# Splitting the first load of an unpooling kernel's indices into two DMAs

## The chip, the cores and the metric

The kernel runs on one core of one Trainium2 chip. The metric is device time in microseconds (us), the median of several executions. Two kernels that are compared by a ratio ran side by side on one chip; the experiments used four chips in all (numbers 11, 10, 3 and 9). The profiler's span starts at the first instruction shown and is about 1.3 us shorter than the time (70.2 against 71.51 us in the profiled run of the kernel before).

## The reference

It is a max-unpooling by 2. Each input value goes to one of the four places of a 2 x 2 output block; the index, 0 to 3, says which. The other three places are zero.

```python
x:       (16, 64, 32, 32) float32
indices: (16, 64, 32, 32) integers 0..3   (64-bit when they reach the kernel)
output = zeros((16, 64, 64, 64), float32)
out_i = i * 2 + idx // 2
out_j = j * 2 + idx % 2
output[b, c, out_i, out_j] = x[b, c, i, j]
```

4.19 MB of x and 8.39 MB of indices are read, 16.78 MB are written.

## The kernel before

A partition holds T = 8 images of N = 1024 values. Three loads are issued first, all on SyncE's queue: three images of indices (24 KB per partition), all of x (32 KB), five images of indices (40 KB).

```python
FIRST = 3
cut = FIRST * 2 * N          # an index is two 32-bit words
program.first(
    nc.sync.dma_start(out=idx_t[:, :cut], in_=idx_v[:, :cut]).then_inc(
        idx_in[0], 16
    )
)
program.first(nc.sync.dma_start(out=x_t, in_=x_v).then_inc(x_in, 16))
program.first(
    nc.sync.dma_start(out=idx_t[:, cut:], in_=idx_v[:, cut:]).then_inc(
        idx_in[1], 16
    )
)
```

VectorE waits for x, then for the first indices (and at the fourth image for the others). For each place of the 2 x 2 block one operation computes (index == place) * x, over one or two images (n below). Two images are one group; four groups are stored, one DMA of 4 MB each, again on SyncE's queue. The last group reuses the output buffer of the first, so it waits for the first store.

```python
nc.vector.wait_ge(x_in, 16).then_inc(x_in, -16)
for t in range(T):
    g, k = t // G, t % G
    if t in (0, FIRST):
        half = int(t == FIRST)
        nc.vector.wait_ge(idx_in[half], 16).then_inc(idx_in[half], -16)
    ...
    if g == NG - 1:
        nc.vector.wait_ge(stored_0, 16).then_inc(stored_0, -16)
    ...
    for pidx in range(4):
        op = nc.vector.scalar_tensor_tensor(
            out=o_c[:, k : k + n, :, pidx // 2, :, pidx % 2],
            in0=idx_c[:, t : t + n],
            scalar=pidx,
            in1=x_c[:, t : t + n],
            op0=mybir.AluOpType.is_equal,
            op1=mybir.AluOpType.mult,
        )
    if k + n == G:
        op.then_inc(made, 1)

for g in range(NG):
    nc.sync.wait_ge(made, g + 1)
    nc.sync.dma_start(out=out_v[g], in_=out_t[g]).then_inc(
        stored if g else stored_0, 16
    )
```

Of the kernel before, what the change touches and what calls it, by code (L numbers as in the profile page):

```python
# [1 line left out]

# [4 lines left out]

P = 128
F32 = mybir.dt.float32
I32 = mybir.dt.int32  # L10


class Program:




    def __init__(self, nc):
        self.nc = nc
        self.block = nc.main_func.blocks[0]  # L20
        self.kernel_block = nc.cur_bb.bb.name

    def __enter__(self):
        ins = self.block.instructions
        self.branches = [i for i in ins if "Branch" in type(i).__name__]
        n = len(ins) - len(self.branches)
        assert all("Branch" in type(ins[k]).__name__ for k in range(n, len(ins)))
        del ins[n:]
        self.nc.switch_bb(self.block.name, parent=None)
        self.symbolic = self.nc._always_lower_symbolic_ap  # L30
        self.nc._always_lower_symbolic_ap = False
        return self

    def first(self, made):
        ins = self.block.instructions
        assert ins[len(ins) - 1].name == made.ins.name
        moved = ins.pop()
        at = next(
            k
            for k, i in enumerate(ins)  # L40
            if i.engine == moved.engine and isinstance(i, mybir.InstDrain)
        )
        ins.insert(at, moved)

    def last(self, made):


        def move(nc):
            ins = self.block.instructions
            at = next(k for k, i in enumerate(ins) if i.name == made.ins.name)  # L50
            nc.main_func.blocks[-1].instructions.append(ins.pop(at))

        self.nc.at_finalize(move)

    def __exit__(self, kind, *_):
        self.nc._always_lower_symbolic_ap = self.symbolic
        if kind is None:
            for b in self.branches:
                self.block.instructions.append(b)
            self.nc.switch_bb(self.kernel_block, parent=None)  # L60


@with_exitstack
def kernel(
    ctx: ExitStack,
    tc: tile.TileContext,
    x: bass.AP,
    indices: bass.AP,
    kernel_size: bass.AP,
    out: bass.AP,  # L70
):
    nc = tc.nc
    assert kernel_size == 2

    B, C, H, W = x.shape
    n_img = B * C
    T = n_img // P
    assert T * P == n_img and C % T == 0

    G = 2  # L80
    NG = T // G
    FIRST = 3
    N = H * W
    x_v = x.rearrange("b (ch t) h w -> (b ch) (t h w)", t=T)
    idx_v = indices.rearrange("b (ch t) h w -> (b ch) (t h w)", t=T).bitcast(I32)
    out_v = out.rearrange("b (ch g t) oh ow -> g (b ch) (t oh ow)", g=NG, t=G)

    x_t = nc.alloc_sbuf_tensor("x_t", [P, T * N], F32).ap()
    idx_t = nc.alloc_sbuf_tensor("idx_t", [P, T * 2 * N], I32).ap()
    out_t = [  # L90
        nc.alloc_sbuf_tensor(f"out_t{g}", [P, G * 4 * N], F32).ap()
        for g in range(NG - 1)
    ]
    out_t.append(out_t[0])

    x_in = nc.alloc_semaphore("x_in")
    idx_in = [nc.alloc_semaphore(f"idx_in{g}") for g in range(2)]
    made = nc.alloc_semaphore("made")
    stored_0 = nc.alloc_semaphore("stored_0")
    stored = nc.alloc_semaphore("stored")  # L100

    x_c = x_t.rearrange("p (t i j) -> p t i j", t=T, j=W)
    idx_c = idx_t.rearrange("p (t i j two) -> p t i j two", t=T, j=W, two=2)[
        :, :, :, :, 0
    ]
    cut = FIRST * 2 * N

    with Program(nc) as program:
        program.first(
            nc.sync.dma_start(out=idx_t[:, :cut], in_=idx_v[:, :cut]).then_inc(  # L110
                idx_in[0], 16
            )
        )
        program.first(nc.sync.dma_start(out=x_t, in_=x_v).then_inc(x_in, 16))
        program.first(
            nc.sync.dma_start(out=idx_t[:, cut:], in_=idx_v[:, cut:]).then_inc(
# [6 lines that stand above are left out]
            g, k = t // G, t % G  # L123
            if t in (0, FIRST):
                half = int(t == FIRST)
                nc.vector.wait_ge(idx_in[half], 16).then_inc(idx_in[half], -16)  # L126


            if k == 1 and t != FIRST and g:
                continue  # L130
            n = 1 if k == 1 or t + 1 == FIRST or not g else 2
            if g == NG - 1:
                nc.vector.wait_ge(stored_0, 16).then_inc(stored_0, -16)
            o_c = out_t[g].rearrange(
                "p (m i two j wo) -> p m i two j wo", m=G, two=2, wo=2, j=W
# [18 lines that stand above are left out]
        nc.sync.sem_inc(made, -NG)  # L154
        program.last(
            nc.sync.wait_ge(stored, 16 * (NG - 1)).then_inc(stored, -16 * (NG - 1))
        )


# [1 line left out]
_INS = ['x', 'indices', 'kernel_size']  # L161
_OUTS = [((16, 64, 64, 64), 'float32')]

_NUMBERS = {'kernel_size': 2}


# [26 lines left out]
```

## Time and profile before

| What | Value |
|---|---|
| time, median of 3 runs before the prediction | 71.60 us |
| span of the profiled run | 70.2 us |
| DMA engines: share of 16 engines' span | 97.6% |
| VectorE busy | 35.9 us, 51% |
| bytes moved | 29.36 MB |
| last load landed / last store landed | 31.4 / 70.2 us |

Read it as one queue: loads, then stores, one after the other on the same 16 DMA engines (mean landings at 9.42, 19.13 and 31.25 us for the loads, 40.95 to 69.93 for the stores). The profile's lines stand in the prediction. Besides the views, the prediction and the text below use the trace's single records: each DMA packet with its start, duration and size, and each landing, which is the moment when one of the 16 engines reports that its part of a DMA is done. A DMA has 16 landings (112 for the seven DMAs of the kernel before); "lands at" means the mean of the 16 unless the last is named.

### The profile page before, as it was taken

How to read it: one execution, taken by the hardware profiler on the slowest of the kernel's cores; microseconds unless marked ns; L12 is line 12 of the kernel's file. 1: busy time of each engine (PE TensorE's matmuls, PEld its weight loads, DVE VectorE, ACT ScalarE, POOL GpSimd, SP SyncE). 2: the span in 40 equal slices, each digit the busy share in tenths (PEclk: the TensorE clock that was granted, in tenths of full speed). 3: DMA queues.
4: the chain of work that ended last, by engine and by line, in shares of the span. 5: the costliest groups of instructions: out<-in, count | busy, mean ns of one | idle time of the engine just before them, and what ended most of it. 6: DMA issues, size and time to landing. Idle time of an engine off the chain costs nothing.

```text
span 70.2 us, 76 instructions
## 1 busy us (share of the span) xinstructions
DVE 35.9 (51%) x24; POOL 0.2 (0%) x4
## 2 busy tenths in 40 slices
DVE  0000000000089999999999999999999500000000
POOL 1000000000000000000000000000000000000000
DMA  7699996979988899869999796969799896969692
GB/s 210 294 406 434 448 598 299 560 336 467 504 373 373 373 584 537 373 299 504 392 411 486 317 579 299 598 299 579 317 467 429 373 523 299 598 299 598 299 486 112
DMA packets 1008, 29.36 MB, mean 418 GB/s; under 512 B 112, under 2 KB 112, under 8 KB 112
## 3 DMA queue, kind: packets, MB, share of 16 engines
q1 hardware_dynamic: 1008, 29.36, 97.6%
HBM read 12.58 MB, written 16.78 MB: 418 GB/s over the span
## 4 chain that ended last, share of the span: by engine, by line
DVE 46%; DVEq 4%; issue 1%
DVE out_t L138 46%; DVEq L188 4%
## 5 line engine op out<-in xcount | busy, mean ns | idle before, releaser
L138 DVE SCALAR_TENSOR_TENSOR out_t<-idx_t,x_t 128x1024 f32<-128x1024 int32 (+1 forms) x24 | 35.9, 1574 | 19.6 <-DVEq L126 19.6
L174 POOL MEMSET const-bfloat16-1.0<- 128x1 bf16 x1 | 0.1, 101 | 0.0
L174 POOL MEMSET const-uint8-127<- 128x1 uint8 x1 | 0.1, 101 | 0.0
L174 POOL MEMSET const-float32-0.0<- 128x1 f32 x1 | 0.1, 98 | 0.2 <-issue 0.2
L174 POOL MEMSET const-float32-1.0<- 128x1 f32 x1 | 0.1, 98 | 0.0
## 6 DMA issues: line engine op xcount, KB each, us to landing
out_dram<-out_t SPq DMA_DIRECT2D x4, 4096.0 KB, 13.4
idx_t<-in_indices_dram SPq DMA_DIRECT2D x1, 5120.0 KB, 30.5
x_t<-in_x_dram SPq DMA_DIRECT2D x1, 4096.0 KB, 18.9
idx_t<-in_indices_dram SPq DMA_DIRECT2D x1, 3072.0 KB, 9.6
```

The costliest lines, as they stand in the source:

```text
L138: op = nc.vector.scalar_tensor_tensor(out=o_c[:, k : k + n, :, pidx // 2, :, pidx % 2], in0=idx_c[:, t : t + n], scalar=pidx, in1=x_c[:, t ...
L174: nc = _bacc.Bacc("TRN2", target_bir_lowering=False, num_devices=1)
L188: with _tile.TileContext(nc) as tc:
```

## The change

The intent is that the first data come in smaller pieces. The first load becomes two: one image (8 KB rows) and two images (16 KB rows). Both raise the same semaphore, each by 16, so the wait is for 32.

```diff
-        program.first(
-            nc.sync.dma_start(out=idx_t[:, :cut], in_=idx_v[:, :cut]).then_inc(
-                idx_in[0], 16
+        for part in (slice(0, 2 * N), slice(2 * N, cut)):
+            program.first(
+                nc.sync.dma_start(out=idx_t[:, part], in_=idx_v[:, part]).then_inc(
+                    idx_in[0], 16
+                )
             )
-        )
...
-                nc.vector.wait_ge(idx_in[half], 16).then_inc(idx_in[half], -16)
+                n_in = 16 if half else 32
+                nc.vector.wait_ge(idx_in[half], n_in).then_inc(idx_in[half], -n_in)
```

## The prediction

> **What bounds the kernel now.** I read the page first for the busy shares. VectorE, the only engine that computes, is busy half the span; the 16 DMA engines are busy nearly all of it.
>
> ```profile
> DVE 35.9 (51%) x24; POOL 0.2 (0%) x4
> ...
> DMA packets 1008, 29.36 MB, mean 418 GB/s; under 512 B 112, under 2 KB 112, under 8 KB 112
> ## 3 DMA queue, kind: packets, MB, share of 16 engines
> q1 hardware_dynamic: 1008, 29.36, 97.6%
> ```
>
> What to see: the queue's packets fill 97.6% of 16 engines' span, 0.976 x 70.2 = 68.5 us, so only about 1.7 us of the span is not filled. The page's chain of waits names VectorE for 46%, but it does not follow the data of the stores, which are what ends the program; it is not the chain to work with here.
>
> Second, the issues and their landings, which give the order in which the one queue is worked off.
>
> ```profile
> out_dram<-out_t SPq DMA_DIRECT2D x4, 4096.0 KB, 13.4
> idx_t<-in_indices_dram SPq DMA_DIRECT2D x1, 5120.0 KB, 30.5
> x_t<-in_x_dram SPq DMA_DIRECT2D x1, 4096.0 KB, 18.9
> idx_t<-in_indices_dram SPq DMA_DIRECT2D x1, 3072.0 KB, 9.6
> ```
>
> What to see: the three loads are issued at 0.00, 0.43 and 0.91 us (timeline below) and land at 9.6, 0.43 + 18.9 = 19.3 and 0.91 + 30.5 = 31.4 us. They are worked off one after the other, not side by side: 9.6 us for 3 MB, 9.7 for 4 MB, 12.1 for 5 MB. From the trace's own landing records (mean over the 16 engines), the loads land at 9.42, 19.13 and 31.25 us and the four stores at 40.95, 50.61, 60.28 and 69.93: one store each 9.66 us, which is 4.194 MB / 9.66 us = 434 GB/s, without a hole from 9.4 us on.
>
> Third, the timeline, to see whether the queue ever runs dry because a store is issued late, and how the head looks.
>
> ```profile
> 0.00 0.38 SPq L110 DMA_DIRECT2D idx_t<-in_indices_dram  x1
> ...
> 0.43 0.43 SPq L114 DMA_DIRECT2D x_t<-in_x_dram  x1
> 0.91 0.43 SPq L116 DMA_DIRECT2D idx_t<-in_indices_dram  x1
> 19.56 35.87 DVE L138 SCALAR_TENSOR_TENSOR out_t<-idx_t,x_t 128x1024 f32<-128x1024 int32 x24 [19.56 <-DVEq L126]
> 28.76 27.03 SPq L151 DMA_DIRECT2D out_dram<-out_t  x4
> ```
>
> What to see: VectorE starts at 19.56 us, when x has landed; the first indices landed 10 us before. The first store is issued at 28.76 us, while the last load's packets run until 31.02 us; the next stores are issued at 37.84, 46.65 and 55.46 us (the records behind the merged row), each while the store before still runs. So VectorE has slack and the stores follow the loads without a gap.
>
> Fourth, the single DMA packets in the trace. A packet is one row of one partition: 24,576 bytes take 912 ns, 32,768 take 1213, 40,960 take 1514. A line through the ends is (1514 - 912) / 16384 = 0.0367 ns per byte, plus 912 - 24,576 x 0.0367 = about 9 ns per packet; it gives the 1213 of the middle one too. A semaphore packet of 4 bytes also takes 9 ns, with a gap of 6. Each of 16 engines moves 8 rows of each DMA: 8 x (912 + 1213 + 1514) + 32 x 1213 = 67.93 us, which is 97% of the span. The rest, worked out for the mean engine: its first packet starts at 1.25 us (the first at 1.03, the last at 1.82); that first packet takes on average about 0.54 us more than 912 ns (1.00 to 1.78 us); seven semaphore packets cost 7 x 15 ns = 0.1 us. 1.25 + 0.54 + 67.93 + 0.10 = 69.8, against a measured mean last landing of 69.93. Outside the span lie another 71.6 - 70.2 = 1.4 us, which no kernel edit of this kind touches.
>
> So the kernel is a DMA queue at line rate plus a head of some 1.8 us, and only the head is within reach of this change.
>
> [...]
>
> **The change part by part.** It removes one DMA of 128 rows of 24 KB and adds one of 128 rows of 8 KB and one of 128 rows of 16 KB, same bytes, same place in the queue. The order of instructions on VectorE is unchanged (16 small and 8 large operations); SyncE has one DMA issue more, and the wait for the first indices is for 32 instead of 16.
>
> Per engine, packets: an 8 KB row by my line is 8192 x 0.0367 + 9 = 310 ns (the trace has 8 KB instruction-fetch packets of 307), a 16 KB row 611. 8 x (307 + 611) = 7344 ns against 8 x 912 = 7296: plus 48 ns. One semaphore packet more: plus 15 ns. In the queue: plus 0.06 us, on the path.
>
> SyncE: one issue more of 0.38 to 0.43 us with a 0.05 us gap, so the loads of x and the late indices are issued about 0.45 us later, at about 0.9 and 1.4. Off the path: the first two DMAs give the engines 7.3 us of work from about 1.8 us on, and x is needed in the queue at about 9 us. The barrier that SyncE joins after its issues moves from 1.67 to about 2.1 us; VectorE waits for x until 19.3 anyway. Cost 0.
>
> Between the two halves: the second DMA is issued at about 0.43 us; the engines' first descriptors came 1.03 to 1.82 us after the first issue, so by about 1.5 to 2.3 us the second set is there. The 8 KB rows last until about 1.8 + 2.5 = 4.3 us. No hole.
>
> The head: the first packets' excess of 0.54 us. First packets that start at 1.03 us take 1.7 us, those that start at 1.8 only 1.0; all end at 2.5 to 2.9 us. So the data begins to flow at about 1.6 to 2.0 us on every engine, whenever its record starts, which looks like a start-up that all share and that does not depend on the row. If so the change wins 0 here; if the excess grows with the first row it shrinks to a third, and 0.36 us are won.
>
> Sum: +0.06 us and a possible -0.36 us.
>
> **The rivals.** First, the head shrinks: for it speaks that the excess sits in the first packets alone and that these are the longest of their kind; against it that the late starters have almost no excess (1004 - 912 = 92 ns) at the same 24 KB. Time 71.6 + 0.06 - 0.36 = 71.3. Second, small rows run worse than the line says, say 30 ns more on each of the 16 packets: 71.6 + 0.06 + 0.5 = 72.1; against it the 307 ns record for 8 KB. Third, the first indices come earlier or later and VectorE with them: hidden anyway, since they have 10 us in hand before x, so 0. Fourth, the store chain gets a hole: the first store is issued 2.26 us before the last load's packets end, and it would have to be issued after about 30 us (31.02 less the 1.03 us from issue to first packet) to leave one; both ends of that margin hang on the loads' landing and move together. Time up to 72.5, very unlikely.
>
> **Range and chances.** The central case is 71.66 (no effect in the head), weight about two thirds; the head shrinking, wholly or partly, about 71.3, one third: mean 71.55. The runs before spread 0.1 us, so a range of 71.2 to 71.85 holds both with some noise. To be over 2% faster takes 1.43 us, more than the 0.54 us of excess and most of the head that is issue time and stays; over 2% slower takes a hole that nothing opens. Each 2%.
>
> **What would show it.** Right: packets 1152 (128 data and 16 semaphore packets more), DMA share again near 97 to 98%, first packets 8 KB long with the data beginning at 1.6 to 2.0 us, both halves of the first indices landed by about 9.5 us, VectorE's start near 19.6, the four stores 9.66 us apart, span 70.0 to 70.3. The head shrinks: x lands 0.3 us earlier and every later landing by the same. Small rows costly: 8 KB packets over 330 ns or gaps between them, first indices after 9.8. Wrong altogether: landings between stores that are no longer 9.66 us apart, or a wait of the queue for VectorE.

A paragraph that leaned on general figures and rules, which no trace of this case shows, has been cut from the prediction, and no term of its sum went with it: 71.6 + 0.06 = 71.66 us with a weight of two thirds, 71.6 + 0.06 - 0.36 = 71.3 with one third, mean 71.55. What went with it is the argument that nothing is to be won in the middle of the queue. Shown are the 434 GB/s per store and 67.93 us of packets in a span of 70.2; that no faster rate exists was not. That the wait for 32 is safe is shown only as a correct result of the changed kernel, in its run beside the experiments.

Where the prediction and the expectations say that a DMA's descriptors come or are there, read that its packets can start: the records show packets alone, and in the kernel before the first ones started 1.03 to 1.82 us after the first issue. When the second DMA's packets can start is the estimate from that.

## The result

The changed kernel took 71.54 us (6 runs, 71.43 to 71.62), the kernel before 71.57 us (6 runs). The ratio is 0.9996, with a 95% interval of 0.9983 to 1.001. Ratios here are the mean time of one kernel's runs over that of the other's of the same rounds, so they are not quite the ratio of the medians quoted. The measured time lies 0.01 us from the predicted 71.55 us, and "within 2%" held.

The page of the changed kernel, queue view:

```profile
DMA packets 1152, 29.36 MB, mean 418 GB/s; under 512 B 128, under 2 KB 128, under 8 KB 128
## 3 DMA queue, kind: packets, MB, share of 16 engines
q1 hardware_dynamic: 1152, 29.36, 97.6%
```

There are 144 packets more, the 128 data packets and 16 semaphore packets that were forecast, at the same bytes, mean rate and share. Next, the issues: what, issuing queue, how many, KB each, us from issue to landing.

```profile
out_dram<-out_t SPq DMA_DIRECT2D x4, 4096.0 KB, 13.5
idx_t<-in_indices_dram SPq DMA_DIRECT2D x1, 5120.0 KB, 30.1
x_t<-in_x_dram SPq DMA_DIRECT2D x1, 4096.0 KB, 18.4
idx_t<-in_indices_dram SPq DMA_DIRECT2D x1, 2048.0 KB, 9.1
idx_t<-in_indices_dram SPq DMA_DIRECT2D x1, 1024.0 KB, 4.7
```

and the timeline of the changed kernel (start us, duration us, engine, line, operation):

```profile
0.00 0.86 SPq L111 DMA_DIRECT2D idx_t<-in_indices_dram  x2
...
0.90 0.43 SPq L115 DMA_DIRECT2D x_t<-in_x_dram  x1
1.38 0.65 SPq L117 DMA_DIRECT2D idx_t<-in_indices_dram  x1
19.50 35.87 DVE L140 SCALAR_TENSOR_TENSOR out_t<-idx_t,x_t 128x1024 f32<-128x1024 int32 x24 [19.50 <-DVEq L128]
28.70 27.03 SPq L153 DMA_DIRECT2D out_dram<-out_t  x4
```

The loads are issued 0.47 us later, and the shorter times from issue to landing (18.4 for 18.9 us, 30.1 for 30.5) are only that. In absolute time nothing moved:

| lands at (mean of 16), us | before | after |
|---|---|---|
| first image of indices | - | 4.50 |
| all first indices | 9.42 | 9.39 |
| x | 19.13 | 19.11 |
| other indices | 31.25 | 31.24 |
| stores | 40.95, 50.61, 60.28, 69.93 | 40.93, 50.60, 60.27, 69.92 |
| very last landing | 70.16 | 70.18 |

### The profile page after: what moved, and what is told of

Read it like the earlier page. It is cut to its first block, busy times and chain, and to the rows that moved or that the text cites. A ratio compares the mean times of both kernels' runs of the same rounds, so it can differ in the third digit from the quotient of the medians.

```text
span 70.2 us, 77 instructions
## 1 busy us (share of the span) xinstructions
DVE 35.9 (51%) x24; POOL 0.2 (0%) x4
## 3 DMA queue, kind: packets, MB, share of 16 engines
q1 hardware_dynamic: 1152, 29.36, 97.6%
## 4 chain that ended last, share of the span: by engine, by line
DVE 46%; DVEq 4%; issue 1%
DVE out_t L140 46%; DVEq L190 4%
## 6 DMA issues: line engine op xcount, KB each, us to landing
idx_t<-in_indices_dram SPq DMA_DIRECT2D x1, 5120.0 KB, 30.1
x_t<-in_x_dram SPq DMA_DIRECT2D x1, 4096.0 KB, 18.4
```

## The experiments

**Theory.** The one DMA queue sets the end. It runs at line rate (434 GB/s per store in the kernel before) behind a head of fixed length (some 1.8 us), so the split adds some 0.06 us of packets. Rivals: the end is set by VectorE and loads are hidden; small rows or more DMAs cost much more and something hid it; the head depends on the first row or on the issuing. All edits are against the changed kernel unless they say otherwise. The kernel before, run beside them, had medians of 71.52 us beside the experiments with 8 KB rows throughout, 1 KB rows, two queues and sixteen partitions; 71.47 beside half the VectorE work, the two shorter loads and four images; 71.45 beside 2 KB rows, 4 KB rows and the changed kernel once more; 71.44 beside itself. Each experiment has one profile, so what is read from single records below is one execution's, while the times are medians of four to six.

### All indices in 8 KB rows

```diff
-        for part in (slice(0, 2 * N), slice(2 * N, cut)):
+        for part in (slice(k * 2 * N, (k + 1) * 2 * N) for k in range(FIRST)):
...
+        for k in range(FIRST, T):           # five DMAs in place of one
+            part = slice(k * 2 * N, (k + 1) * 2 * N)
...
-                n_in = 16 if half else 32
+                n_in = 16 * (T - FIRST) if half else 16 * FIRST
```

> All eight images of the indices are loaded in 8 KB rows by eight DMAs. Theory (queue at line rate, a fixed cost per packet and per DMA): 8 KB packets follow each other every 306 ns and 40 KB packets every 1511, so a packet costs about 5 ns beside its bytes; against the kernel before there are 48 more data packets per engine (0.24 us) and six more semaphore packets of 15 ns (0.09 us): +0.33 us, 71.9. Rival (small rows or more DMAs cost far more, and the change only hid it): +1 us or more. Rival (the loads' end is hidden behind VectorE): 0.

Measured: 71.93 us, ratio 1.0068 (1.0055 to 1.0081), so +0.41 us, with a correct result. The issues view:

```profile
idx_t<-in_indices_dram SPq DMA_DIRECT2D x8, 1024.0 KB, 20.8
x_t<-in_x_dram SPq DMA_DIRECT2D x1, 4096.0 KB, 18.0
```

The images land 2.48 us apart (x lies between the third and the fourth); 8 x 306 ns and 6 ns for the semaphore packet are 2.45, and the rest are packets a little longer than usual. The last indices land at 31.59 us, 0.34 later than before, and the last store at 70.26, 0.33 later: a delay in the loads is passed on whole to the end. Loads are not hidden. Six more DMAs than in the kernel before cost about what their packets cost. The profile fell on the fastest of the six runs (71.83), so in the median the cost is nearer 0.4 us than 0.33.

### Half the work on VectorE

```diff
-        for t in range(T):
+        for t in range(T // 2):
...
-            nc.sync.wait_ge(made, g + 1)
-            nc.sync.dma_start(out=out_v[g], in_=out_t[g]).then_inc(
+            nc.sync.wait_ge(made, min(g, 1) + 1)
+            nc.sync.dma_start(out=out_v[g], in_=out_t[g % 2]).then_inc(
```

The wait for the first store is moved from VectorE to the end of SyncE's program. The result is wrong.

> Wrong result on purpose: VectorE computes only images 0 to 3, and the last two stores write the first two outputs again; loads and stores keep all their bytes. Theory (the DMA queue sets the end, VectorE has slack): 71.5, no change. Rival (the page's chain of waits through VectorE sets the end): VectorE is done some 17 us earlier and the time falls by several us.

Measured: 71.53 us against 71.47, ratio 1.0004 (0.9988 to 1.0021). The page of this run:

```profile
DVE 18.3 (26%) x16; POOL 0.2 (0%) x4
...
q1 hardware_dynamic: 1152, 29.36, 97.3%
```

VectorE lost 17.6 us of work and the time did not move. The stores land at 60.28 and 69.93 us, as before. The page's chain of waits, which names VectorE, does not name the bound here.

### Half an image less to load

```diff
-            nc.sync.dma_start(out=idx_t[:, cut:], in_=idx_v[:, cut:]).then_inc(
+            nc.sync.dma_start(out=idx_t[:, cut : 15 * N], in_=idx_v[:, cut : 15 * N]).then_inc(
...
-                    in0=idx_c[:, t : t + n],
+                    in0=idx_c[:, min(t, 5) : min(t, 5) + n],
```

The result is wrong.

> Wrong result on purpose: the last load leaves out half an image (36 KB rows instead of 40), 0.52 MB less of 29.36. Theory: 0.52 MB / 434 GB/s = 1.21 us less, if the first store's descriptors are in the queue before the loads run out (load end 31.1 - 1.2 = 29.9, issue at 28.7): 70.3. Rival (loads are hidden): 71.5.

Measured: 70.80 us, ratio 0.9904 (0.989 to 0.9919), so -0.67 us, about half of what was expected. The last load does land early, at 30.12 us, 1.12 sooner than in the changed kernel. But the first store is issued at 28.70 us and its first packet starts only at 29.63, when the quickest engines have been out of work since 29.51. The first store lands 9.88 us after the last load, not 9.69, and the next three take 9.74, 9.73 and 9.71 in place of 9.67, 9.67 and 9.65: -1.12 + 0.19 + 0.19 = -0.74. The condition in the expectation was not met: the store's first packet comes 0.93 us after its issue, and that is too late for the quickest engines. The issue in the timeline:

```profile
28.70 27.03 SPq L153 DMA_DIRECT2D out_dram<-out_t  x4
```

### A whole image less to load

The same edit with `14 * N`; the result is wrong.

> Wrong result on purpose: the last load leaves out a whole image (32 KB rows), 1.05 MB less. Theory: 2.42 us less of queue, but then the loads' packets end at 28.7 us, when the first store is only being issued; with 0.6 to 1.0 us from issue to its first packet a hole of that size opens and 1.4 to 1.8 us are won: 69.7 to 70.1. Without a hole: 69.1. Rival (loads are hidden): 71.5.

Measured: 70.54 us, ratio 0.9873 (0.9858 to 0.9887), so -0.93 us, where -1.4 to -1.8 was expected. Its timeline has the first store late, and the windows (us, VectorE busy and instructions, GpSimd the same, granted clock, DMA share, GB/s) show an empty queue:

```profile
29.00 27.03 SPq L153 DMA_DIRECT2D out_dram<-out_t  x4
```

```profile
28.00:29.00 1.00, 1.00 (x2) 0.00 (x0) 1.00 0.01 0
29.00:30.00 1.00, 1.00 (x1) 0.00 (x0) 1.00 1.22 524
```

(The windows book a packet where it starts, so the 1.22 belongs to packets that begin at 29.85 us and reach past 30.) The single records give it exactly: the loads' packets end at 28.35 us on average, the store is issued at 29.00 and its packets start at 29.85 to 30.00. Of the 2.47 us by which the last load lands sooner, 1.57 go to that hole and 0.22 to the three later stores. That leaves 0.68 us in the mean landing and 0.84 in the very last one.

My expectation was too good in two places: the hole begins 0.35 us earlier than I had put it, since I had counted from the last engine's last packet (31.11 us in the changed kernel) and the mean engine ends sooner, and the store was issued 0.3 us later, because VectorE starts when the slowest of 16 engines has landed x (19.55 us), not the mean one (19.07).

### Four images before x

```diff
-    FIRST = 3
+    FIRST = 4
```

> Four images instead of three before x (8 KB and 24 KB rows). Theory: x lands 2.42 us later, VectorE starts at 21.9 us, the first store is issued at 31.1 us while the loads still end at 31.1; a hole of 0.6 to 1.0 us: 72.1 to 72.5. Rival (the loads' order and VectorE's start do not matter): 71.5.

Measured: 72.94 us, ratio 1.0202 (1.0177 to 1.0227), correct result, and 0.4 us above the expected range. The edit also lets VectorE take the third and fourth image together (20 operations instead of 24), but the first store's operations stay as they were: it is issued 9.20 us after VectorE's start in both kernels. First its issue and the windows of this run, then those of the changed kernel:

```profile
31.39 26.75 SPq L153 DMA_DIRECT2D out_dram<-out_t  x4
```

```profile
30.00:31.00 1.00, 1.00 (x2) 0.00 (x0) 1.00 0.01 0
31.00:32.00 1.00, 1.00 (x2) 0.00 (x0) 1.00 0.00 0
32.00:33.00 1.00, 1.00 (x1) 0.00 (x0) 1.00 1.22 524
```

```profile
30.00:31.00 1.00, 1.00 (x2) 0.00 (x0) 1.00 1.15 492
31.00:32.00 1.00, 1.00 (x1) 0.00 (x0) 1.00 0.61 262
32.00:33.00 1.00, 1.00 (x2) 0.00 (x0) 1.00 0.68 295
```

Here x lands 2.39 us later, the first store is issued at 31.39, and no new packet starts from 31 to 32 us. The last load lands at the same time (31.21), the first store 1.52 us later after it than in the changed kernel, and the three others together 0.20 us slower: the mean last landing is 71.61 us. The hole is larger than the expected 0.6 to 1.0 us for the two reasons just told: the loads' packets end at 30.78 us on average, not 31.1, and the store is issued at 31.39, not 31.1, with its packets starting at 32.23 to 32.38. So the order of the loads does matter; the kernel's choice of three images sits about 1 us from a hole.

### The first piece in 1 KB, 2 KB and 4 KB rows

```diff
-        for part in (slice(0, 2 * N), slice(2 * N, cut)):
+        for part in (slice(0, N // 4), slice(N // 4, cut)):      # 1 KB and 23 KB rows
```

and likewise `N // 2` (2 KB and 22 KB) and `N` (4 KB and 20 KB).

> The first load is split in 1 KB rows and 23 KB rows. Theory (start-up that all engines share, whatever the row): the data flows at the same moment, +0.06 us against before, 71.6. Rival (the first packet's excess grows with its row): the 0.54 us of excess fall to almost nothing, 71.1. Second rival: 128 KB do not last until the second DMA's descriptors are there (issued 0.43 us later), a hole of up to 0.4 us: 72.0.

> The first load is split in 2 KB rows and 22 KB rows. 8 rows of 2 KB last about 0.65 us, until about 1.75 us, while the second DMA's descriptors come at about 1.5 to 2.2 us. Theory (excess grows with the row, and a gap costs): 71.4 to 71.5. Rival (shared start-up): 71.6. Second rival (the excess comes again at the second DMA): 71.65.

> The first load is split in 4 KB rows and 20 KB rows. The runs so far gave an excess of the first packets of 0.54 us at 24 KB, 0.43 at 8 KB and 0.02 at 1 KB. Theory (the excess grows with the first row, as long as the second DMA's descriptors come in time: 8 rows of 4 KB last 1.2 us): about 0.2 us of excess, 0.34 won against before, 0.06 lost on packets: 71.25. Rival (start-up that all engines share): 71.55 to 71.6. Second rival (the excess comes again at the second DMA's first packets, as with the 1 KB rows): 71.6 or more, seen in 20 KB packets longer than 765 ns.

Measured: 1 KB 71.67 us, ratio 1.0023 (1.0011 to 1.0035); 2 KB 71.64 us, ratio 1.0038 (1.0016 to 1.0061); 4 KB 71.98 us, ratio 1.0076 (1.0063 to 1.0089). None is a win. The expected gains (71.1 with 1 KB rows, 71.4 to 71.5 with 2 KB, 71.25 with 4 KB) did not come, and 4 KB rows cost more than either rival had named as a figure; their five runs lie at 71.96 to 72.05. In the single records I took, for each DMA, how much longer its packets are than the usual duration of their size, summed and divided by 16 engines:

| Profile | first packet starts (mean of 16 engines), us | excess in the first DMA, us | excess in the second DMA, us | sum | of the sum, in packets that start before 2.5 us |
|---|---|---|---|---|---|
| before, 24 KB rows | 1.26 | 0.54 | 0.00 | 0.54 | 0.54 |
| changed, 8 KB then 16 KB | 1.23 | 0.47 | 0.00 | 0.47 | 0.47 |
| 1 KB then 23 KB | 1.17 | 0.05 | 0.52 | 0.57 | 0.55 |
| 2 KB then 22 KB | 1.20 | 0.19 | 0.37 | 0.56 | 0.37 |
| 4 KB then 20 KB | 1.21 | 0.49 | 0.36 | 0.85 | 0.49 |

(The records don't name the engine. Where the rows are short, the first start is worked out from the 16 semaphore packets that close the DMA: their mean start, less eight packets and the excess.)

With 1 KB rows the data flows at once: the first packets start at 0.99 to about 1.3 us and take mostly 44 to 60 ns. But the excess is not gone. It is paid by the 23 KB packets right behind, which start at 1.5 to 2.2 us and take up to 1571 ns in place of 874. Besides, the engines stand idle for 0.18 us on average between the two DMAs, which is part of the hole that the second rival named; with 2 KB and 4 KB rows there is none. So about half a microsecond (0.37 to 0.55 here) is paid by whatever packets pass before 2.5 us, whether the first rows are 1, 2, 4, 8 or 24 KB. Another count says the same: with each packet's bytes spread evenly over its record, 0.33 to 0.42 MB have passed by 2.5 us in all twelve profiles that load 128 rows from SyncE's queue alone.

The rest of the sum with 2 KB and 4 KB rows (0.19 and 0.36 us) is not the start-up: it lies in packets of the second DMA that start from 2.5 to 6.8 us. With 4 KB rows 44 of the second DMA's 128 packets run more than 5% long. That is what makes 4 KB rows dearer: the first indices land at 9.77 us, 0.35 later than before. Why these packets run long stays open. Such stretches of long packets come elsewhere too: from 19.6 to 24.5 us in the run with half an image less.

### Two issuing queues

```diff
-        for part in (slice(0, 2 * N), slice(2 * N, cut)):
+        for eng, part in ((nc.sync, slice(0, 2 * N)), (nc.scalar, slice(2 * N, cut))):
             program.first(
-                nc.sync.dma_start(out=idx_t[:, part], in_=idx_v[:, part]).then_inc(
+                eng.dma_start(out=idx_t[:, part], in_=idx_v[:, part]).then_inc(
```

> The 16 KB part of the first indices is issued from ScalarE's queue while SyncE issues the 8 KB part; x follows on SyncE 0.43 us sooner than in the changed kernel. Theory: the queue's head is set by the time from the first issue to the first data, so 71.55, within 0.15 us. Rival (the issue rate of one sequencer sets the head): 0.2 to 0.4 us faster.

Measured: 72.03 us, ratio 1.0073 (1.0055 to 1.0091), so +0.51 us where 0 was expected; the rival, a gain, failed too. The profile fell on the slowest of the six runs (72.23). The issues view:

```profile
idx_t<-in_indices_dram ACTq DMA_DIRECT2D x1, 2048.0 KB, 13.9
idx_t<-in_indices_dram SPq DMA_DIRECT2D x1, 1024.0 KB, 8.5
```

The two queues are worked off side by side: the 8 KB rows land at 7.81 us rather than 4.50, and the 16 KB rows at 13.29 rather than 9.39. The mean landing of x is 0.25 us later than in the changed kernel, and its last engine lags 0.70 us behind the mean. That lag is there from the first DMA on (last landing 8.52, mean 7.81) and stays to the end (70.87 against a mean of 70.16). Issuing earlier gained nothing: the first packets start at the same time (1.23 us), and ScalarE's queue, whose DMA is issued at 0.12 us, has its first packet only at 2.79. Why it waits is not shown.

### Sixteen partitions first

```diff
-        for part in (slice(0, 2 * N), slice(2 * N, cut)):
+        for rows in (slice(0, 16), slice(16, P)):
             program.first(
-                nc.sync.dma_start(out=idx_t[:, part], in_=idx_v[:, part]).then_inc(
+                nc.sync.dma_start(out=idx_t[rows, :cut], in_=idx_v[rows, :cut]).then_inc(
```

> The first load is split by partitions: 16 rows first (one per engine), then 112 rows, all of 24 KB. Theory: start-up does not depend on the number of rows in the first DMA either; +0.015 us for one DMA more, 71.6. Rival (the staggered start of the engines, 1.03 to 1.82 us[...]): engines start within 0.1 us of each other and the time falls by up to 0.4 us, 71.2.

Measured: 78.25 us, ratio 1.0935 (1.0914 to 1.0957): far outside both. The windows:

```profile
1.00:6.00 5.00, 0.00 (x0) 0.00 (x0) 1.00 1.17 211
6.00:16.00 10.00, 0.00 (x0) 0.00 (x0) 1.00 0.97 261
16.00:26.00 10.00, 0.00 (x0) 0.00 (x0) 1.00 1.00 433
```

The engines are full (share 0.97) but move 261 GB/s until the first indices have landed, and 433 as soon as x with its 128 rows begins. The first DMA, 0.39 MB, lands at 5.30 us, 4.0 us after its packets start (1.31). The packet records alone are shorter: they take 2.4 us on average and end at 3.71, and the landing comes 1.6 us after that, where the first load of the kernel before needs 0.36. Why the DMAs of 16 and of 112 rows run slower than those of 128 was not shown. On the head the run answers one thing: with one packet per engine the starts still spread from 1.00 to 1.81 us, against 1.03 to 1.82 with 128 rows in the kernel before, so the spread doesn't come from the number of rows.

### The two kernels once more

> The changed kernel once more, beside the two above. All theories: 71.5 to 71.6, first packets of 8 KB with about 0.4 us of excess.

> The kernel before against itself, for the scatter of the head from one profile to the next and of the ratio. Theory (a start-up of about half a microsecond is paid once by whatever packets pass first): ratio 1.00 within 0.2%, and the 24 KB first packets again 0.4 to 0.6 us longer than 912 ns on average. Rival (the 0.54 us of the one profile was an accident and the 24 KB rows start as well as the small ones): an excess clearly under the 0.26 to 0.51 us that 8 KB rows showed.

Measured: the changed kernel 71.56 us, ratio 1.0026 (1.000 to 1.0051), with two of its six runs at 71.81 and 72.08; the kernel before against itself 71.48 us, ratio 1.0005 (0.9993 to 1.0017). The profile of the changed kernel fell on the 72.08 run. There 16 of the 40 KB packets ran more than 5% long, most of them starting from 28.9 to 29.5 us, and one or a few engines finished late: the last landing (70.73) is 0.66 us behind the mean (70.06), while in the other profile it was 0.26. It is not caused by the first load, whose indices landed earlier than usual (9.22 us); what caused it stays open. The excess of the 24 KB packets was 0.58 us in the second profile of the kernel before. The seven profiles that begin with 8 KB rows on SyncE's queue alone show 0.26, 0.44, 0.46, 0.46, 0.47, 0.50 and 0.51 us in the first DMA, on average 0.44.

## Why the prediction was right

**The number.** That 71.54 us fell within 0.01 of 71.55 is luck. 71.55 is the average of two cases, 71.66 and 71.3, and nothing was expected to take just that time. The measured change is -0.03 us (-0.12 to +0.07): it rules out the -0.30 us of the shrinking head, and it can't tell the central +0.06 from nothing.

**The bound.** "A DMA queue at line rate plus a head" was shown from three sides: 17.6 us less VectorE work changed nothing, 0.34 us more in the loads came out whole at the last store (0.33), and fewer bytes made it faster. The limit of this was shown as well: with four images before x, VectorE's later start opens a hole and costs 1.5 us.

**The sum of the time.** The prediction's 69.8 us met the mean last landing of 69.93 partly by luck. The records overlap by 3 to 4 ns (a packet of 912 ns is followed 908 ns after its start), which is 0.2 us over 56 packets, and a semaphore packet is followed 6 ns after its start, not 15. So the sum is 69.6 us, and that is where the mean engine's packets end (69.57); the landing comes 0.35 us later, which the sum had left out. The two errors nearly cancel, and neither differs between the kernels.

**The added packets.** The predicted +48 and +15 ns are too small to be seen in a time. The starts of packets give about +40 and +6 ns: 8 x (306 + 607) against 8 x 908, and 6 for the semaphore packet. With all indices in 8 KB rows the working, over five times as large, met the landings (+0.33 and +0.34 us), but not term by term: packets and semaphores add 0.27 us by the records, the head's excess was 0.11 smaller, and the later small packets ran 0.14 long in sum. The cost of a packet beside its bytes is nearer 5 ns than the 9 of my line, since packets 309 ns long follow each other every 306. The 307 ns that the prediction took for 8 KB were those of three of seven instruction-fetch packets; the others took 324 to 541. The rows' median of 309 ns bears the guess out.

**The extra issue on SyncE.** It moved the other loads' issues by 0.47 us, and neither x's landing nor VectorE's start (19.50 us) went with it: off the path, as said.

**The head.** The size was about right, one sentence of the reasoning was not. "A start-up that all share and that does not depend on the row" holds as a sum: the 0.54 and 0.58 us of the 24 KB rows stand against 0.26 to 0.51, on average 0.44, with 8 KB rows, so about 0.1 us is won, not the 0.36 of the rival, and the packets take half of it back. But "the data begins to flow at about 1.6 to 2.0 us on every engine" is wrong, and with it one of the signs that the prediction named for being right: in the changed kernel one 8 KB packet has ended at 1.44 us, and with 1 KB rows data flows from about 1.0 us on. I had taken a slow first packet for a late one. The runs show a cost of about half a microsecond that falls on the packets passing before 2.5 us; its mechanism was not settled. One rival that no run was made for is that issuing further loads slows the packets. The run with eight loads of indices speaks against it: its issues go on until 4.6 us, and its packets that start from 2.5 to 4.5 us have only 0.02 us of excess.

**The margin before the first store.** I put the latest issue at about 30 us, from the end of the last packet and 1.03 us from issue to packet. The runs with a hole show 0.85 to 0.93 us from a store's issue to its first packet, and the first engine of the kernel before runs out at 30.66 us, so the limit is 30.66 - 0.93 = 29.7 and the margin 1.0 us behind the issue at 28.76. The change doesn't touch it, so the forecast was not hurt.

**The chances.** Being faster by 2% needed 1.43 us and the whole head's excess is 0.5. No run here found a version with a correct result that beats the kernel before.

## What to carry to other kernels

Here one queue's packets filled 97.6% of the span, and cutting a load that stayed in this queue cost 0.06 us of packets by the working and could win back at most the 0.54 us of excess in the head: -0.03 us (-0.12 to +0.07) was measured. Add up the packets before trying such a change. Take the margin of the first store from the first engine that runs dry (30.66 us in the kernel before, the last one at 31.02) and from the last engine that lands x (19.31 us, the mean at 19.13), not from means. Before believing that a slow first packet is a property of that packet, make it small and look whether the cost moves to the next (with 1 KB rows 0.05 us stayed in the first DMA and 0.52 came in the second), and look when each long packet starts, since not all of them belong to the start (0.36 us with 4 KB rows came from 2.5 us on).
